# Layer 1's activation rows: low part first, a gap between the parts, rows 2560 bytes apart, and low weights displaced by 128 bytes

## The chip, the cores and the metric

The kernel runs on one core of one Trainium2 chip. The metric is the device time of one execution in microseconds; the kernel before took 2322.99 us (median of three runs, 2322.8 to 2323.42). A profile is one execution recorded by the hardware.

## The reference

A small decoder trunk on 256 tokens with 16 learned prefix tokens in front (272 rows in all), width 2048, two layers, in fp32:

```python
h = jnp.concatenate([meta, x], axis=1)                       # 272 x 2048
# layer 0: forgetting attention
proj = rms_norm(h, norm_attn[0]) @ fox_w_in[0]               # q, k, v, forget gates
h = h + forgetting_attention(q, k, v, cum_logf) @ fox_w_o[0]
h = h + squared_relu_mlp(rms_norm(h, norm_mlp[0]), w_up[0], w_down[0])   # 2048 -> 8192 -> 2048
# layer 1: stick-breaking attention over one shared K/V
k_s, v_s = split(rms_norm(h, kv_norm) @ w_kv)
q = rms_norm(h, norm_attn[1]) @ sb_w_q[0]
h = h + stick_breaking_attention(q, k_s, v_s) @ sb_w_o[0]
h = h + squared_relu_mlp(rms_norm(h, norm_mlp[1]), w_up[1], w_down[1])
out = rms_norm(h, final_norm)[:, 16:]                        # the prefix is dropped
```

Nearly all the arithmetic is in the projections, each an activation matrix times a weight matrix that is read once from memory.

## The kernel before

Activations lie transposed: a feature chunk of 128 features fills the 128 partitions, and the tokens run along a row. There are 16 chunks. Layer 0 works on all 272 tokens. In layer 1 the prefix is needed only for the keys and values, so all its other projections work on 256 tokens; in the code `t0` is 0 for the first kind and 16 (`M`) for the second.

Each fp32 product is made of three products of a faster type, float32r: activations and weights are split into a high part (rounded) and a low part (the rest), and high x high, high weight x low activation, and low weight x high activation are added up; low x low is left out. The class `Split` (L119) holds one such activation matrix: one tile `x_...` of 16 rows per partition, one row for each chunk, with the high and the low part of the chunk in it. `ROWS` (L28) says, in elements of 4 bytes, how far apart rows are and where the parts start: in layer 0 rows are 640 elements apart, the high part starts at 48 and the low part at 368; with 256 tokens rows are 576 apart, the high part starts at 16 and the low part at 272, directly behind it.

`gemm_group` (L182) makes 512 output features of one projection: four accumulators of 128 features, 16 chunks of weights in four blocks `kb` of four chunks. Weights come by DMA into `raw` (two chunks each), ScalarE rounds them into `whi` (L217), VectorE subtracts to get `wlo` (L218). The pool of the weights' parts holds four buffers of each; TensorE then runs the products.

- With all 272 tokens there are three products of 272 elements for each chunk and accumulator (L247 to L249).
- With 256 tokens (`pairs`) the two products with the high weights are one: `sp.both` moves the high and the low activations, 512 elements, in one instruction, and fills the whole accumulator bank of 512 columns, high in the first half and low in the second (L237). The product with the low weights moves the 256 high activations and adds to the first half (L241). At the end `evac` gets both halves and adds them (`residual_add` L254, `total` L258). One accumulator at the very end of layer 1's MLP (`apart`) is made in the first manner.

In blocks 0 and 3 a group runs accumulator by accumulator: four products of 512, then four of 256. In blocks 1 and 2 it runs eight of 512, then eight of 256. Every product loads its weights anew, and the load for the next product runs beside the present one. `gemm_matmul` (L174) pins the order in which products are issued.

All products of all projections are recorded under line L176 of the profile; the accumulator is `acc`, and the names tell the operands: `acc<-x_m,whi` is a high weight by an activation of the up projection, `x_u` the down projection, `x_o` the attention's output projection, `x_a` the first norm's, `x_kv` the shared keys and values.

Where tiles lie: a pool `align` with one tile of 128 bytes stands between the raw weights and their parts. With it `whi`, `wlo` and both `x` buffers begin at multiples of 256 bytes in each partition. An `x` tile is 16 x 640 + 64 elements long, whatever its pitch, and the pool has two buffers of it.

Of the kernel before, what the change touches and what calls it, by code (L numbers as in the profile page):

```python
# [10 lines left out]
F32R = mybir.dt.float32r  # L11
# [4 lines left out]
P = 128  # L16
D = 2048
NC = D // P
M = 16
# [4 lines left out]
QSCALE = 1.0 / math.sqrt(P)  # L24
N_FF = 4


ROWS = {0: (640, 48, 368), M: (576, 16, 272)}  # L28
XROW = 640

G_A0, G_M0, G_KV, G_A1, G_M1, G_FIN = range(6)
# [3 lines left out]
def yoco_kernel(ctx: ExitStack, tc: tile.TileContext, hT_in, gains, b_f, w_f, w_qkv0, w_o0, w_up, w_dn,  # L35
# [7 lines left out]
    wspl = ctx.enter_context(tc.tile_pool(name="wspl", bufs=4))  # L43
# [75 lines left out]
    class Split:  # L119


        def __init__(self, label, t0):
            n = T - t0
            self.t0 = t0
            rows = xs.tile([P, NC * XROW + 64], F32R, tag="x", name=f"x_{label}")
            pitch, hi, lo = ROWS[t0]
            rows = rows[:, hi:hi + NC * pitch].rearrange("p (c t) -> p c t", c=NC)
            self.hi, self.lo = rows[:, :, :n], rows[:, :, lo - hi:lo - hi + n]
            self.both = rows[:, :, :2 * n]

    def split_chunk(sp, gi, c):

# [41 lines left out]
    def gemm_matmul(*args, **kw):  # L174

        ins = nc.tensor.matmul(*args, **kw).ins  # L176
        if queued and pinned[0]:
            tc.add_manual_dep(ins, queued[0].name, mybir.DependencyInfo(mybir.DependencyClass.NoSync,
                                                                        mybir.DependencyReason.DATA))
        queued[:] = [ins]  # L180

    def gemm_group(wblk, sp, t0, evac, before={}, after={}, load_x=None, pairs=False, apart=()):  # L182

        uid[0] += 1
        u = uid[0]
        accs = [pacc.tile([P, 512], F32, tag="acc", name=f"acc_{u}_{m}") for m in range(4)]  # L190
        n = T - t0
        for kb in range(4):
            src_w = wblk[kb].rearrange("p (k c) -> p k c", k=4)
            if kb in before:
                before[kb]()
            piece = 1 if load_x is not None and kb < 2 else 2
            raws = [wraw.tile([P, 2, 512], F32, tag="raw", name=f"raw_{u}_{kb}_{hf}") for hf in range(2)]
            for k0 in range(0, 4, piece):
                if load_x is not None:
                    load_x(range(4 * kb + k0, 4 * kb + k0 + piece))  # L200
                if load_x is not None and kb == k0 == 0:

                    for c0 in (0, 256):
                        nc.scalar.dma_start(raws[0][:, 0, c0:c0 + 256], src_w[:, 0, c0:c0 + 256])
                else:
                    nc.sync.dma_start(raws[k0 // 2][:, k0 % 2:k0 % 2 + piece], src_w[:, k0:k0 + piece])
            parts = []
            for hf in range(2):
                whi = wspl.tile([P, 2, 512], F32R, tag="whi", name=f"whi_{u}_{kb}_{hf}")
                wlo = wspl.tile([P, 2, 512], F32R, tag="wlo", name=f"wlo_{u}_{kb}_{hf}")  # L210
                boxes = [(o, piece, 0, 512) for o in range(0, 2, piece)]
                if load_x is not None and kb == hf == 0:
                    boxes[:1] = [(0, 1, 0, 256), (0, 1, 256, 512)]
                for o, no, c0, c1 in boxes:
                    src = raws[hf][:, o:o + no, c0:c1]
                    hp, lp = whi[:, o:o + no, c0:c1], wlo[:, o:o + no, c0:c1]
                    on_act = nc.scalar.activation(hp, src, AF.Copy)  # L217
                    on_dve = nc.vector.tensor_tensor(out=lp, in0=src, in1=hp.bitcast(F32), op=ALU.subtract)  # L218
                parts.append((whi, wlo))
            if kb in after:  # L220
                with tc.issue_after(on_act.ins), tc.issue_after(on_dve.ins):
                    after[kb]()


            if load_x is not None and kb == 0:
                runs = [([kc], range(4)) for kc in range(4)]
            elif kb in (0, 3):
                runs = [(range(4), [m]) for m in range(4)]
            else:
                runs = [(range(2 * hf, 2 * hf + 2), range(4)) for hf in range(2)]  # L230
            pinned[0] = load_x is None
            for kcs, ms in runs:
                paired = [m for m in ms if pairs and m not in apart]
                single = [m for m in ms if m not in paired]
                for kc in kcs:
                    for m in paired:
                        gemm_matmul(accs[m], parts[kc // 2][0][:, kc % 2, m * P:(m + 1) * P], sp.both[:, 4 * kb + kc],  # L237
                                    start=kb == kc == 0, stop=False)
                for kc in kcs:
                    for m in paired:  # L240
                        gemm_matmul(accs[m][:, :n], parts[kc // 2][1][:, kc % 2, m * P:(m + 1) * P],  # L241
                                    sp.hi[:, 4 * kb + kc], start=False, stop=kb == kc == 3)
                for m in single:
                    for kc in kcs:
                        wh, wl = (w[:, kc % 2, m * P:(m + 1) * P] for w in parts[kc // 2])
                        hi, lo = sp.hi[:, 4 * kb + kc], sp.lo[:, 4 * kb + kc]
                        gemm_matmul(accs[m][:, :n], wh, hi, start=kb == kc == 0, stop=False)  # L247
                        gemm_matmul(accs[m][:, :n], wh, lo, start=False, stop=False)
                        gemm_matmul(accs[m][:, :n], wl, hi, start=False, stop=kb == kc == 3)  # L249
                if kb == 3:  # L250
                    for m in ms:
                        evac(m, [accs[m][:, :n]] + ([accs[m][:, n:]] if m in paired else []))
# [18 lines left out]
    def load_x(chunks):  # L271
        c0, n = chunks[0], len(chunks)
        nc.sync.dma_start(hT[:, c0:c0 + n, :], hT_in[:, c0:c0 + n, :])
        if c0 == 0:
            nc.sync.dma_start(g_sb, gains)
        for c in chunks:
            split_chunk(xa, G_A0, c)
# [86 lines left out]
    for g in range(4):  # L364
# [11 lines left out]
        if g == 0:  # L376

            gemm_group(w_qkv0[0], xa, 0, lambda m, acc, qT=qT: nc.scalar.copy(qT[:, m, :], acc[0]),
                       after={kb: (lambda kb=kb: first_norm(kb)) for kb in range(4)}, load_x=load_x)
            gate_products()  # L380
            box["rstd"] = norm.finish()
            for m in range(4):
                evac_q(m, [qT[:, m, :]])
            forget_gates(box["rstd"])
        else:
            gemm_group(w_qkv0[3 * g], xa, 0, evac_q)
# [4 lines left out]
        def decays(j):  # L391

            for i, (o, n) in enumerate(((0, 144), (144, T))):
                nc.vector.scalar_tensor_tensor(out=s[:, j, o:o + n], in0=fk[:, j, :n],
                                               scalar=fq_sb[:, i, 4 * g + j:4 * g + j + 1],
                                               in1=maskA[:, o:o + n], op0=ALU.subtract, op1=ALU.add)

        gemm_group(w_qkv0[3 * g + 1], xa, 0, lambda m, acc: evac_kv(m, acc, kT),
                   after={j: (lambda j=j: decays(j)) for j in range(4)})

# [255 lines left out]
    a, y, t, rs = (fin[:, i, :] for i in range(4))  # L656
# [81 lines left out]
```

## Time and profile before

| | |
|---|---|
| median of three runs | 2322.99 us (2322.8 to 2323.42) |
| profiled execution | 2323.63 us |
| its span, first to last instruction | 2321.9 us |
| TensorE busy | 2310.8 us |
| VectorE busy | 1350.6 us |
| ScalarE busy | 1064.0 us |
| read from memory | 407.29 MB |
| mean granted TensorE clock | 0.998 |

Span and profiled time differ by 1.7 us, the start and the end outside the instructions. In the rows of the profile PE is TensorE, PEld its weight loads, DVE VectorE, ACT ScalarE. A row of a group names line, engine, operation, output and inputs, their sizes, the count, then busy time in us with the mean duration in ns, then the engine's idle time just before these instructions with what ended it. Matmuls overlap in the pipeline, so the pace is read from the distance of starts in the timeline, or from the number of matmuls in a window.

### The profile page before, as it was taken

Reading aid. Unit: us, or ns where it says so; the run is one execution under the profiler, and the core shown is the slowest. Engines: PE = TensorE matmul, PEld = TensorE weight load, DVE = VectorE, ACT = ScalarE, POOL = GpSimd, SP = SyncE. Lnnn points to the kernel's source line nnn. Section 1 sums busy time; section 2 is a strip of 40 time slices with the busy share of each in tenths; the row PEclk is TensorE's granted clock in tenths of the full one; section 3 lists DMA queues with packets and bytes.
Section 4 is the critical chain, followed back from the end, with each engine's and each line's share of the span. In section 5 each row is a group of like instructions: output and inputs, shape, how many; then the busy total and the mean of one; then the engine's idle time right before and its main releaser. Section 6 shows DMA issues by size and latency. Waiting matters only on the chain.

```text
span 2321.9 us, 39954 instructions
## 1 busy us (share of the span) xinstructions
PE 2310.8 (100%) x16486; PEld 2190.4 (94%) x16486; DVE 1350.6 (58%) x1923; ACT 1064.0 (46%) x1477; POOL 39.9 (2%) x58
## 2 busy tenths in 40 slices
PE   9999999999999999999999999999999999999998
PEld 9999999999999999999998999988888888888887
DVE  7665555655455455445566655567665665665665
ACT  6434344544344344344455444455544543543553
POOL 1000000000000000000000000000000000000000
PEclk9999999999999999999999999999999999999999
DMA  6544444455555455555556444455555555556553
GB/s 233 172 156 165 171 158 173 171 183 173 183 175 183 171 186 176 178 182 171 187 173 200 155 145 146 146 175 186 197 184 193 192 186 198 186 184 199 181 199 127
DMA packets 116630, 412.00 MB, mean 177 GB/s; under 512 B 13264, under 2 KB 16736, under 8 KB 116448
## 3 DMA queue, kind: packets, MB, share of 16 engines
q1 hardware_dynamic: 114560, 406.29, 51.4%
q10 hardware_dynamic: 1888, 3.16, 0.4%
q8 instruction: 129, 2.11, 0.4%
q14 instruction: 53, 0.43, 0.1%
HBM read 407.29 MB, written 2.11 MB: 176 GB/s over the span
## 4 chain that ended last, share of the span: by engine, by line
PE 99%; DMA 0%; DVE 0%; ACT 0%; issue 0%; DVEq 0%; SPq 0%; ACTq 0%
PE acc L176 95%; PE ps L406 0%; PE pza L585 0%; PE pv L339 0%; PE po L468 0%; PE po L624 0%; DMA raw<-w_qkv 0%; PE po L625 0%; PE pzb L586 0%; PE po L469 0%; DMA hT<-hT_in 0%; PE po L626 0%; DVE ob L680 0%; PE pf L306 0%; PE pf L305 0%; PE pta L600 0%
## 5 line engine op out<-in xcount | busy, mean ns | idle before, releaser
L218 DVE TENSOR_TENSOR wlo<-raw,whi 128x1024 fp32r<-128x1024 f32 (+1 forms) x773 | 931.5, 1217 | 746.8 <-ACT whi L217 745.2
L217 ACT ACTIVATE whi<-raw 128x1024 fp32r<-128x1024 f32 (+1 forms) x773 | 799.2, 1050 | 953.9 <-PE acc L176 877.4
L176 PE MATMUL acc<-x_u,whi 128*128 128x272 f32 (+2 forms) x3088 | 647.5, 321 | 0.0
L176 PE MATMUL acc<-x_m,whi 128*128 128x272 f32 (+1 forms) x3072 | 646.1, 322 | 0.0
L176 PEld LDWEIGHTS acc<-x_u,whi 128*128 128x128 f32 x3088 | 499.9, 188 | 26.7
L176 PEld LDWEIGHTS acc<-x_m,whi 128*128 128x128 f32 x3072 | 497.8, 188 | 27.4
L176 PE MATMUL acc<-x_u,wlo 128*128 128x272 f32 (+1 forms) x2048 | 445.9, 282 | 0.0
L176 PE MATMUL acc<-x_m,wlo 128*128 128x272 f32 (+1 forms) x2048 | 443.7, 282 | 0.0
L176 PE MATMUL acc<-x_a,whi 128*128 128x272 f32 (+1 forms) x1792 | 360.6, 306 | 0.4 <-ACT x_a L134 0.2
L176 PEld LDWEIGHTS acc<-x_u,wlo 128*128 128x128 f32 x2048 | 340.3, 188 | 15.7
L176 PEld LDWEIGHTS acc<-x_m,wlo 128*128 128x128 f32 x2048 | 339.5, 188 | 15.9
L176 PEld LDWEIGHTS acc<-x_a,whi 128*128 128x128 f32 x1792 | 284.4, 188 | 9.9 <-issue 0.7
L176 PE MATMUL acc<-x_a,wlo 128*128 128x272 f32 (+1 forms) x1024 | 254.5, 286 | 0.0
L176 PE MATMUL acc<-x_kv,whi 128*128 128x272 f32 x1024 | 194.1, 288 | 0.0
L176 PEld LDWEIGHTS acc<-x_a,wlo 128*128 128x128 f32 x1024 | 179.6, 188 | 4.9 <-issue 0.5
L176 PE MATMUL acc<-x_o,whi 128*128 128x272 f32 (+1 forms) x768 | 162.3, 322 | 0.0
L176 PEld LDWEIGHTS acc<-x_kv,whi 128*128 128x128 f32 x1024 | 160.6, 188 | 0.4
L176 PE MATMUL acc<-x_kv,wlo 128*128 128x272 f32 x512 | 147.3, 288 | 0.0
L256 DVE TENSOR_TENSOR hT<-acc,hT 128x256 f32<-128x256 f32 (+1 forms) x239 | 102.4, 428 | 71.4 <-PE acc L176 69.5
L176 PEld LDWEIGHTS acc<-x_o,whi 128*128 128x128 f32 x768 | 124.3, 188 | 6.8
L176 PE MATMUL acc<-x_o,wlo 128*128 128x272 f32 (+1 forms) x512 | 111.6, 283 | 0.0
L176 PEld LDWEIGHTS acc<-x_kv,wlo 128*128 128x128 f32 x512 | 96.5, 188 | 0.1
(226 smaller groups left out, 1040.0 us busy)
## 6 DMA issues: line engine op xcount, KB each, us to landing
raw<-w_up SPq DMA_DIRECT2D x256, 512.0 KB, 4.7
raw<-w_dn SPq DMA_DIRECT2D x256, 512.0 KB, 4.7
raw<-w_qkv SPq DMA_DIRECT2D x92, 512.0 KB, 3.8
raw<-w_o SPq DMA_DIRECT2D x64, 512.0 KB, 4.5
raw<-w_kv SPq DMA_DIRECT2D x64, 512.0 KB, 3.6
raw<-w_q SPq DMA_DIRECT2D x32, 512.0 KB, 4.6
fk<-f_dram ACTq DMA_DIRECT2D x4, 544.0 KB, 5.0
raw<-w_qkv SPq DMA_DIRECT2D x7, 256.0 KB, 4.8
```

What stands on the lines that cost most here:

```text
L176: ins = nc.tensor.matmul(*args, **kw).ins
L217: on_act = nc.scalar.activation(hp, src, AF.Copy)
L218: on_dve = nc.vector.tensor_tensor(out=lp, in0=src, in1=hp.bitcast(F32), op=ALU.subtract)
L256: nc.vector.tensor_tensor(out=hT[:, c, t0:], in0=a, in1=hT[:, c, t0:], op=ALU.add)
```

## The change

For layer 1's matrices with 256 tokens the low part now comes first, at the row's start (element 0), and the high part starts at element 304, so that a gap of 48 elements lies between them; rows are 640 elements (2560 bytes) apart, as in layer 0. The paired product moves two pieces of 256 elements. Its accumulator now has the low activations' half first, and the low weights' product adds to the second half. A buffer of `wlo` has rows of 576 elements instead of 512; in groups with pairs the 512 weights start 32 elements (128 bytes) into the row, in the others at its beginning. Layer 0's `ROWS` keep their places. The pool of the weights' parts grows by 4 x 512 bytes, and everything allocated behind it moves up by 2048 bytes.

```diff
-ROWS = {0: (640, 48, 368), M: (576, 16, 272)}
+ROWS = {0: (48, 368), M: (304, 0)}
 XROW = 640
...
-            pitch, hi, lo = ROWS[t0]
-            rows = rows[:, hi:hi + NC * pitch].rearrange("p (c t) -> p c t", c=NC)
-            self.hi, self.lo = rows[:, :, :n], rows[:, :, lo - hi:lo - hi + n]
-            self.both = rows[:, :, :2 * n]
+            hi, lo = ROWS[t0]
+            o = min(hi, lo)
+            rows = rows[:, o:o + NC * XROW].rearrange("p (c t) -> p c t", c=NC)
+            self.hi, self.lo = (rows[:, :, k - o:k - o + n] for k in (hi, lo))
+
+            d = abs(lo - hi)
+            if t0:
+                self.both = rows[:, :, :2 * d].rearrange("p c (i t) -> p c i t", i=2)[:, :, :, :n]
+            self.low_first = lo < hi
...
-                wlo = wspl.tile([P, 2, 512], F32R, tag="wlo", name=f"wlo_{u}_{kb}_{hf}")
+                wlo = wspl.tile([P, 2, 576], F32R, tag="wlo", name=f"wlo_{u}_{kb}_{hf}")
+                wlo = wlo[:, :, 32:544] if pairs else wlo[:, :, :512]
...
-                        gemm_matmul(accs[m][:, :n], parts[kc // 2][1][:, kc % 2, m * P:(m + 1) * P],
+                        gemm_matmul(accs[m][:, n:] if sp.low_first else accs[m][:, :n],
+                                    parts[kc // 2][1][:, kc % 2, m * P:(m + 1) * P],
                                     sp.hi[:, 4 * kb + kc], start=False, stop=kb == kc == 3)
```

## The prediction

> **What bounds the kernel now.** I read the page first (busy times, chain), then TensorE's waits, then the groups by shape, and last the timeline of TensorE, where the pace of single forms shows. The page:
>
> ```profile
> span 2321.9 us, 39954 instructions
> ...
> PE 2310.8 (100%) x16486; PEld 2190.4 (94%) x16486; DVE 1350.6 (58%) x1923; ACT 1064.0 (46%) x1477; POOL 39.9 (2%) x58
> ...
> PE 99%; DMA 0%; DVE 0%; ACT 0%; issue 0%; DVEq 0%; SPq 0%; ACTq 0%
> ```
>
> TensorE is busy from end to end, and 99% of the chain that ended last is its own work. Its whole waiting, in the view of waits of that engine:
>
> ```profile
> PE pr_fin L669 <- DVE fin L663: 1.3, 1, 1.3
> PE idle L62 <- DVE mean_w L58: 1.1, 1, 1.1
> PE pms_fin L637 <- ACT sq_fin L649: 0.2, 1, 0.2
> PE acc L176 <- ACT x_a L134: 0.2, 1, 0.2
> ```
>
> That is 2.8 us, of which 0.2 us lies in the products of L176. So no transfer, split or eviction sets the time; only the pace at which TensorE takes one matmul after another does, and the change can act on the time only through that pace. The groups by shape give the counts of the forms that the change touches, the paired ones (x_m, x_u, x_o, x_a of layer 1; 512 elements moved by a high weight, 256 by a low one), and the two operations that split the weights:
>
> ```profile
> L218 DVE TENSOR_TENSOR wlo<-raw,whi 128x1024 fp32r<-128x1024 f32 x764 | 925.5, 1223 | 744.4 <-ACT whi L217 742.9
> ...
> L176 PE MATMUL acc<-x_m,whi 128*128 128x512 f32 x1024 | 266.8, 393 | 0.0
> L176 PE MATMUL acc<-x_u,whi 128*128 128x512 f32 x1008 | 262.6, 392 | 0.0
> ...
> L176 PE MATMUL acc<-x_u,wlo 128*128 128x256 f32 x1024 | 152.5, 278 | 0.0
> L176 PE MATMUL acc<-x_m,wlo 128*128 128x256 f32 x1024 | 150.4, 278 | 0.0
> ...
> L176 PE MATMUL acc<-x_o,whi 128*128 128x512 f32 x256 | 67.2, 393 | 0.0
> L176 PE MATMUL acc<-x_a,whi 128*128 128x512 f32 x256 | 66.9, 393 | 0.0
> ```
>
> The durations there (393 and 278 ns) overlap, since matmuls are pipelined; the pace has to come from starts. There are 1024 + 1008 + 256 + 256 = 2544 paired products of 512, and one low-weight product of 256 goes with each. The first window below lies in layer 1, the second in layer 0 (us; busy, instructions; clock; DMA):
>
> ```profile
> 1800.00:2200.00 400.00, 400.00 (x2311) 1.00 0.56 190
> 700.00:1100.00 400.00, 400.00 (x3246) 1.00 0.52 179
> ```
>
> In layer 1 one matmul takes 400 / 2311 = 173.1 ns on average, so one pair (a 512 and a 256) 346.2 ns; in layer 0 a 272-wide one takes 400 / 3246 = 123.2 ns. The granted clock is 1.00 in both. The pairs are 2544 x 0.3462 = 881 us, 38% of the span. The timeline of TensorE in one group of layer 1 (start us, length, instructions; the length includes the pipeline's tail, so I use differences of starts):
>
> ```profile
> 1622.00 0.62 PE L176 MATMUL acc<-x_m,wlo 128*128 128x256 f32 x4
> 1622.45 1.07 PE L176 MATMUL acc<-x_m,whi 128*128 128x512 f32 x4
> 1623.37 0.63 PE L176 MATMUL acc<-x_m,wlo 128*128 128x256 f32 x4
> 1623.84 1.09 PE L176 MATMUL acc<-x_m,whi 128*128 128x512 f32 x4
> ...
> 1626.60 2.00 PE L176 MATMUL acc<-x_m,whi 128*128 128x512 f32 x8
> 1628.45 1.10 PE L176 MATMUL acc<-x_m,wlo 128*128 128x256 f32 x8
> 1629.39 2.00 PE L176 MATMUL acc<-x_m,whi 128*128 128x512 f32 x8
> 1631.23 1.11 PE L176 MATMUL acc<-x_m,wlo 128*128 128x256 f32 x8
> ```
>
> Two things are to be seen. Sixteen 512s take 1.85 + 1.84 us, 230.6 ns each, so on average 346.2 - 230.6 = 115.6 ns are left for a 256. And the 256s have two paces in the same code: four in 0.45 us (112.5 ns), then four in 0.47 us (117.5 ns), and eight in 0.94 us (117.5 ns). The pace of a form is thus not fixed, though its rows lie alike; something at its start picks it.
>
> **The change, part by part.** Each engine's instructions stay in number, order and waits; what moves are addresses and the form of some operands.
>
> *Distances of whole 256 bytes.* The pitch of a row goes from 2304 to 2560 bytes (9 and 10 times 256), a wlo slot from 4096 to 4608, and all tiles behind the slots by 2048. The trace holds such a shift: x_m and x_u lie in the pool's two buffers, (16 x 640 + 64) x 4 = 41216 = 161 x 256 bytes apart. The same stretch of a group that reads x_u:
>
> ```profile
> 1737.44 2.00 PE L176 MATMUL acc<-x_u,whi 128*128 128x512 f32 x8
> 1739.28 1.10 PE L176 MATMUL acc<-x_u,wlo 128*128 128x256 f32 x8
> 1740.22 2.00 PE L176 MATMUL acc<-x_u,whi 128*128 128x512 f32 x8
> 1742.06 1.11 PE L176 MATMUL acc<-x_u,wlo 128*128 128x256 f32 x8
> ```
>
> 1.84, 0.94 and 1.84 us, as for x_m. So such shifts cost 0, and layer 0, whose operands move by nothing else, keeps its 123.2 ns.
>
> *The subtraction writes wlo with a gap.* L218 wrote 1024 elements in a row and now writes 2 x 512. A row in which VectorE writes two pieces of 256:
>
> ```profile
> L361 DVE TENSOR_TENSOR x_o<-po,x_o 128x512 fp32r<-128x512 f32 x16 | 11.1, 692 | 20.3 <-ACT x_o L360 20.3
> ```
>
> Two of these are 1384 ns against 1223, so a subtraction costs between 0 and +161 ns. It hides under TensorE: VectorE stood idle 744.4 us before these subtractions, waiting for whi, and TensorE waited for none of them beyond the 0.2 us above. I take 0; without that cover it would be up to 764 x 0.161 = 123 us, but the idle time is six times that.
>
> *Evictions.* The low-weight products now add to the second half of the accumulator, not the first. Both halves are one tile, released by the same last product, so L256, L262 and L263 run at the same times: 0.
>
> *The paired operand is now two pieces.* Before, 512 elements in one run; now 256, a skip of 48 elements, 256. Layer 1's attention moves two pieces of the same type, 416 elements apart:
>
> ```profile
> 1332.15 0.40 PE L600 MATMUL pta<-eh,ntri_r 128*128 128x512 f32 x1
> 1332.38 0.29 PE L604 MATMUL ptb<-eh,ntri_r 128*128 128x288 f32 x1
> ...
> 1333.50 0.40 PE L601 MATMUL pta<-el,ntri_r 128*128 128x512 f32 x1
> 1333.73 0.29 PE L602 MATMUL pta<-eh,nones_r 128*128 128x288 f32 x1
> 1333.86 0.30 PE L603 MATMUL pta<-el,nones_r 128*128 128x288 f32 x1
> 1334.00 0.29 PE L605 MATMUL ptb<-el,ntri_r 128*128 128x288 f32 x1
> 1334.13 0.29 PE L176 MATMUL acc<-x_kv,whi 128*128 128x272 f32 x1
> ```
>
> The 512s take 0.23 us, no more than the unbroken ones to the 10 ns that single rows resolve. The three 288s in a row take 1334.13 - 1333.73 = 0.40 us, 133.3 ns each; an unbroken 288 at layer 0's pace would take 123.2 x 288 / 272 = 130.4 ns. One break then costs 2.9 ns. I take that, since three in a row resolve better than single ones: 2544 x 2.9 ns = +7.4 us. Ends: 0 from the 512s, +7.4 from the 288s.
>
> *Where the rows start against the weights.* Modulo 256 bytes, before: whi and wlo at 0, both activation parts at 64. After: whi at 0, wlo at 128, low part at 0, high part at 192. So a pair starts at 0 against its weights instead of 64, and the low-weight product stays at 64 (192 - 128). No row shows a start at 0. For the 512 the ends are two of the fastest 256s, 225.0 ns (2544 x -5.6 = -14.2 us), and the pace per element of the broken 288s, 133.3 x 512 / 288 = 237.0 ns (+6.4 ns, +16.3 us, the break within it). For the 256 they are the two paces, 112.5 and 117.5 against the mean of 115.6: -7.9 to +4.8 us. Between ends on both sides of the present pace I take 0, the present pace being nearest to both.
>
> [...]
>
> **Sum.** +7.4 us from the break, 0 from the rest. The profiled execution took 2323.63 us (span 2321.9), so it would take 2331.0; the median of the runs is 2322.99, 0.6 us below, so I predict 2330.4 us, +0.32%. A difference of 0.2%, 4.6 us, is about what can be told from no change.
>
> **Rivals.**
>
> *Faster: the fast pace of the low-weight products becomes the rule.* The start of a run picks between 112.5 and 117.5 ns, and new ends of the pairs before it could always pick the first, while a break in mid-operand costs nothing, as the 512s of L600 and L601 have it. That gives 2322.99 - 7.9 = 2315.1 us. For it: both paces occur already, next to each other. Against it: nothing says which start the new pairs leave. It decides against my forecast once the break costs less than 3.1 ns and the fast pace holds throughout. Lower still, with the pairs half way to 225 ns as well (-7.1), lies 2308.
> [...]
>
> *No change.* TensorE reads a row without regard to where it starts, and the skip is free: 2323.0 us, within 4.6 us. For it: the equal times of x_m and x_u, and the 0.23 us of the broken 512s. Against it: equal times were shown for shifts of whole 256 bytes alone. [...]
>
> *Much slower: starting level with the weights collides.* Pair and whi now start at the same place modulo 256, a case that no row has. If each 512 goes at 237.0 ns and each 256 at its slow 117.5: +16.3 + 4.8 = +21.1 us, 2344.1 us. Against it: the next weight load starts alongside every product already, without a wait of TensorE in the profile.
>
> **How the numbers follow.** Forecast (break paid, paces kept) 0.38, with its own range from 2328 to 2335; faster 0.32; no change 0.16; much slower 0.14. A small part of the forecast's case falls under 0.2%: faster 0.32, same 0.17, slower 0.51. The range for 8 in 10 runs from 2311 to 2341: it leaves out the lower tail of the faster case and the most of the much slower one.
>
> **What would show it right or wrong.** After the change, eight 512s of one group in the timeline should take 1.87 us (233.5 ns) where they took 1.85 and 1.84, and the 256s still show 112.5 and 117.5 ns mixed. The window in the middle of layer 1 should count 2292 matmuls in 400 us instead of 2311 (349.1 ns a pair), that of layer 0 still 3246. If the 512s keep 1.84 us, the break is free; if the 256s all run at one pace, the starts matter, which I priced at 0; if layer 0 moves, a shift of whole 256 bytes is not neutral; if TensorE waits for wlo, the gap in the subtraction costs more than its cover. Any of these makes the prediction wrong in the step named.

## The result: 7 us slower, as many as forecast, and not where forecast

The changed kernel takes 2330.04 us (median of 8 runs, 2329.54 to 2331.78) against 2323.02 for the kernel before on the same chip: a ratio of 1.0031, 95% interval 1.0020 to 1.0042. The forecast was 2330.4. The page of the changed kernel, its busy times and its chain:

```profile
span 2330.1 us, 39954 instructions
...
PE 2317.9 (99%) x16486; PEld 2197.0 (94%) x16486; DVE 1351.1 (58%) x1923; ACT 1064.1 (46%) x1477; POOL 39.1 (2%) x58
...
PE 99%; DMA 1%; DVE 0%; ACT 0%; issue 0%; DVEq 0%; ACTq 0%; SPq 0%
```

TensorE is busy 7.1 us longer (2317.9 against 2310.8) and is still 99% of the chain. Its waits in the products:

```profile
PE acc L180 <- ACT whi L222: 1.2, 2, 0.9
...
PE acc L180 <- ACT x_a L138: 0.2, 1, 0.2
```

The 1.2 us are two waits in the first 20 us, in layer 0, that the profile of before does not have. They are part of why this one execution took 2331.78 us, 1.7 above the median. The windows in layers 1 and 0:

```profile
1800.00:2200.00 400.00, 400.00 (x2292) 1.00 0.58 189
700.00:1100.00 400.00, 400.00 (x3245) 1.00 0.54 178
```

Layer 0 keeps its pace (3245 against 3246 matmuls), and layer 1 falls from 2311 to 2292, 349.0 ns a pair. That is the number the prediction named. The groups by shape show that it comes about otherwise:

```profile
L180 PE MATMUL acc<-x_m,whi 128*128 128x512 f32 x1024 | 267.4, 393 | 0.0
L180 PE MATMUL acc<-x_u,whi 128*128 128x512 f32 x1008 | 263.2, 393 | 0.0
L180 PE MATMUL acc<-x_u,wlo 128*128 128x256 f32 x1024 | 154.7, 281 | 0.0
L180 PE MATMUL acc<-x_m,wlo 128*128 128x256 f32 x1024 | 152.6, 281 | 0.0
```

The products that now move two pieces last 393 ns (393 and 392 before). It is the low-weight products, whose operand has no break, that go from 278 to 281 ns. The timeline of the group shown before (same instructions):

```profile
1624.73 0.64 PE L180 MATMUL acc<-x_m,wlo 128*128 128x256 f32 x4
1625.20 1.09 PE L180 MATMUL acc<-x_m,whi 128*128 128x512 f32 x4
1626.13 0.64 PE L180 MATMUL acc<-x_m,wlo 128*128 128x256 f32 x4
1626.61 1.09 PE L180 MATMUL acc<-x_m,whi 128*128 128x512 f32 x4
...
1629.40 2.01 PE L180 MATMUL acc<-x_m,whi 128*128 128x512 f32 x8
1631.25 1.11 PE L180 MATMUL acc<-x_m,wlo 128*128 128x256 f32 x8
1632.19 2.01 PE L180 MATMUL acc<-x_m,whi 128*128 128x512 f32 x8
1634.05 1.11 PE L180 MATMUL acc<-x_m,wlo 128*128 128x256 f32 x8
```

Eight 512s take 1.85 and 1.86 us, not the 1.87 foretold. The runs of four 256s take 0.47 and 0.48 us, where before every other one took 0.45: the fast pace is gone there. Taken over all products in the two traces, as the mean distance from one start to the next, a 512 went from 230.16 to 230.98 ns and a 256 from 116.46 to 118.34: 2544 x 0.82 = 2.1 us and 2544 x 1.88 = 4.8 us, 6.9 us together.

### The profile page after: what moved, and what is told of

It is laid out like the page before. It is cut to its first block, busy times and chain, and to the rows that moved or that the text cites. A ratio compares the mean times of both kernels' runs of the same rounds, so it can differ in the third digit from the quotient of the medians.

```text
span 2330.1 us, 39954 instructions
## 1 busy us (share of the span) xinstructions
PE 2317.9 (99%) x16486; PEld 2197.0 (94%) x16486; DVE 1351.1 (58%) x1923; ACT 1064.1 (46%) x1477; POOL 39.1 (2%) x58
## 4 chain that ended last, share of the span: by engine, by line
PE 99%; DMA 1%; DVE 0%; ACT 0%; issue 0%; DVEq 0%; ACTq 0%; SPq 0%
PE acc L180 95%; DMA hT<-hT_in 1%; PE ps L412 0%; PE pza L591 0%; PE pv L345 0%; PE po L474 0%; PE po L630 0%; PE pzb L592 0%; PE po L631 0%; DMA g_sb<-gains 0%; PE po L475 0%; PE po L632 0%; DVE ob L686 0%; PE pf L311 0%; PE pf L312 0%; PE pta L606 0%
```

## The experiments

All kernels below compute the same function. What they vary are three places modulo 256 bytes, always against the weights loaded for the product: where the first piece of the paired operand starts, where the second piece starts, and where the low-weight product's operand starts (the table gives the three in bytes). Four theories were set against each other. A is the prediction: the break between the pieces costs, the starts do not. B: each product's own start sets its pace. C: unlike starts of the parts cost. D: starts at an even multiple of 64 bytes (0, 128) are dear, at an odd one (64, 192) cheap.

All times are medians, with the ratio to the kernel before in the same batch and its interval (its median was 2323.52 us in the batch of the e runs, 2323.54 in that of the f runs and 2323.30 in that of the g runs and h1); the paces are mean distances of starts over all such products of the trace.

| kernel | first, second, low | us | ratio (95%) | 512, ns | 256, ns |
|---|---|---|---|---|---|
| before | 64, 64, 64 | 2323.02 | | 230.16 | 116.46 |
| changed | 0, 192, 64 | 2330.04 | 1.0031 (1.0020 to 1.0042) | 230.98 | 118.34 |
| e1_break | 64, 64, 64 | 2323.68 | 1.0001 (0.9991 to 1.0010) | 230.16 | 116.46 |
| e4_shift | 64, 64, 64 | 2323.38 | 0.9998 (0.9989 to 1.0008) | 230.15 | 116.46 |
| e2_wlo128 | 64, 64, 192 | 2329.26 | 1.0024 (1.0015 to 1.0034) | 232.29 | 116.62 |
| e3_rows | 0, 192, 192 | 2328.55 | 1.0023 (1.0014 to 1.0032) | 230.24 | 118.29 |
| f1_at0 | 0, 0, 0 | 2333.13 | 1.0040 (1.0026 to 1.0055) | 231.47 | 118.82 |
| f2_at128 | 128, 128, 128 | 2334.94 | 1.0047 (1.0032 to 1.0062) | 231.86 | 119.11 |
| f3_at192 | 192, 192, 192 | 2324.81 | 1.0004 (0.9994 to 1.0014) | 232.67 | 114.35 |
| f4_lo0_hi64 | 0, 64, 64 | 2333.03 | 1.0041 (1.0026 to 1.0056) | 232.83 | 117.46 |
| g1_lo64_hi192 | 64, 192, 192 | 2320.43 | 0.9988 (0.9978 to 0.9997) | 231.95 | 113.49 |
| g2_hi64_lo192 | 64, 192, 64 | 2331.75 | 1.0037 (1.0024 to 1.0050) | 231.85 | 118.05 |
| g3_hi192_lo64 | 192, 64, 192 | 2337.34 | 1.0061 (1.0046 to 1.0076) | 233.14 | 118.84 |
| h1_weights64 | 0, 0, 0 | 2332.34 | 1.0039 (1.0025 to 1.0053) | 231.47 | 118.83 |

### The break alone

```diff
-ROWS = {0: (640, 48, 368), M: (576, 16, 272)}
+ROWS = {0: (640, 48, 368), M: (640, 16, 336)}
```

The paired operand is two pieces with 256 bytes between them; the code that builds it is that of the changed kernel.

> The kernel before with the break alone: high part at 16 as before, low part at 336 behind a gap of 64 elements (256 bytes), rows 640 apart, so every start keeps its place modulo 256 bytes; wlo not displaced. Theory A (the prediction: the break costs 2.9 ns in each of 2544 pairs, the starts nothing): +7.4 us, 2330.4, the 512s at 233.5 ns, the 256s at 115.6 with both paces. Theory B (the starts modulo 256 set the pace, the break is free): 2323.0 within 1 us, all paces as before.

Theory A falls. The timeline of the same group:

```profile
1626.88 2.00 PE L182 MATMUL acc<-x_m,whi 128*128 128x512 f32 x8
1628.73 1.10 PE L182 MATMUL acc<-x_m,wlo 128*128 128x256 f32 x8
1629.67 2.00 PE L182 MATMUL acc<-x_m,whi 128*128 128x512 f32 x8
1631.51 1.11 PE L182 MATMUL acc<-x_m,wlo 128*128 128x256 f32 x8
1632.45 0.39 PE L182 MATMUL acc<-x_m,whi 128*128 128x512 f32 x1
```

1.85, 0.94, 1.84 us and 0.94 to the next run: what the kernel before shows. Over all 2544 pairs a 512 takes 230.16 ns and a 256 116.46 with the break as without it, and the time is 2323.68 us against 2323.52: the break costs nothing.

### Shifts of whole 256 bytes

```diff
-ROWS = {0: (640, 48, 368), M: (576, 16, 272)}
+ROWS = {0: (640, 48, 368), M: (640, 16, 272)}
...
-                wlo = wspl.tile([P, 2, 512], F32R, tag="wlo", name=f"wlo_{u}_{kb}_{hf}")
+                wlo = wspl.tile([P, 2, 576], F32R, tag="wlo", name=f"wlo_{u}_{kb}_{hf}")
+                wlo = wlo[:, :, 0:512]
```

> The kernel before with shifts of whole 256 bytes alone: layer 1's rows 640 elements apart instead of 576, rows of wlo 576 instead of 512 without a displacement, all tiles behind moved by 2048 bytes. Theories A and B both expect 2323.0 within 1 us and every pace as before; if it is slower, addresses above 256 bytes or the written gap of wlo matter.

It came out so: the row pitch of 2560 bytes, the longer wlo slots with the gap that VectorE writes, and the tiles moved by 2048 bytes cost nothing (2323.38 us against 2323.52; 230.15 and 116.46 ns against 230.16 and 116.46).

### The two halves of the change

The displacement of wlo alone, activations as before:

```diff
-                wlo = wspl.tile([P, 2, 512], F32R, tag="wlo", name=f"wlo_{u}_{kb}_{hf}")
+                wlo = wspl.tile([P, 2, 576], F32R, tag="wlo", name=f"wlo_{u}_{kb}_{hf}")
+                wlo = wlo[:, :, 32:544] if pairs else wlo[:, :, 0:512]
```

> The kernel before with wlo alone displaced by 128 bytes in the paired groups (rows of wlo 576 elements), activations as before. The low-weight product then starts at 192 instead of 64 against its weights. Theory A: 2323.0, no change. Theory B: the 256s change their pace, somewhere from 112.5 to 120 ns, so -8 to +11 us; the 512s before another 512 keep 230.6 ns.

And the rows alone, low part first, with wlo at the beginning of its rows of 576 elements (the accumulator's halves change places as in the changed kernel):

```diff
-ROWS = {0: (640, 48, 368), M: (576, 16, 272)}
+ROWS = {0: (640, 48, 368), M: (640, 304, 0)}
```

> The changed kernel without the displacement of wlo: low part at 0, high part at 304, wlo at the beginning of its rows of 576 elements. Theory A: +7.4 us, 2330.4, as in the changed kernel, all of it in the 512s. Theory B: the 512s as in the changed kernel (they see the same starts), the 256s another pace than its 118.4 ns, because they start at 192 instead of 64 against wlo: from 2319 to 2334.

Each is slower by itself, 5.7 and 5.0 us above the 2323.52 of this batch, and the two together by 7.0: they do not add up. With wlo displaced:

```profile
1622.77 0.63 PE L182 MATMUL acc<-x_m,wlo 128*128 128x256 f32 x4
1623.24 1.10 PE L182 MATMUL acc<-x_m,whi 128*128 128x512 f32 x4
1624.17 0.63 PE L182 MATMUL acc<-x_m,wlo 128*128 128x256 f32 x4
...
1627.46 2.03 PE L182 MATMUL acc<-x_m,whi 128*128 128x512 f32 x8
1629.33 1.11 PE L182 MATMUL acc<-x_m,wlo 128*128 128x256 f32 x8
```

The 512s, whose moving rows and own weights had not moved, went from 230.16 to 232.29 ns. Taken by place in the run, over the runs of four and eight in the trace, the last 512 went from 228.6 to 235.8 ns and the others from 230.5 to 231.4. Beside that last one the displaced wlo of the next product is loaded, and it makes up 3.4 of the 5.4 us that all 512s lost. Theory B had the 512s before another 512 unchanged; they moved less, by 0.9 ns, but they moved. So a product's pace depended here on more than its own start. The 256s kept their mean, but only as a mean: for x_m and x_u the runs of four went from 116.1 to 117.9 ns a product, and the runs of eight from 116.8 to 115.2.

With the rows alone, a run of four and a run of eight:

```profile
1621.34 1.08 PE L182 MATMUL acc<-x_m,whi 128*128 128x512 f32 x4
1622.26 0.64 PE L182 MATMUL acc<-x_m,wlo 128*128 128x256 f32 x4
1622.74 1.08 PE L182 MATMUL acc<-x_m,whi 128*128 128x512 f32 x4
...
1626.94 2.00 PE L182 MATMUL acc<-x_m,whi 128*128 128x512 f32 x8
1628.78 1.10 PE L182 MATMUL acc<-x_m,wlo 128*128 128x256 f32 x8
1629.71 2.00 PE L182 MATMUL acc<-x_m,whi 128*128 128x512 f32 x8
```

Four 512s take 0.92 us and four 256s 0.48 us, 120 ns each, slower than either pace of before. Eight 256s take 0.93 us, so the last four of them, in 0.45 us, run at the faster pace again. The 512s keep 230.24 ns, and the 256s carry the whole loss: theory A had it all in the 512s. Theory B expected the 256s at another pace than in the changed kernel, and their mean is the same (118.29 and 118.34 ns).

### Unbroken rows at the other places

One line of each of three kernels (the code that builds the operands is that of e1_break, which for unbroken rows makes the operand of before):

```diff
-ROWS = {0: (640, 48, 368), M: (576, 16, 272)}
+ROWS = {0: (640, 48, 368), M: (576, 0, 256)}
+ROWS = {0: (640, 48, 368), M: (576, 32, 288)}
+ROWS = {0: (640, 48, 368), M: (576, 48, 304)}
```

> The kernel before with layer 1's rows moved 64 bytes down: high part at 0, low part at 256 elements, unbroken, wlo not displaced; every start is 0 modulo 256, like whi and wlo. Theory B (each product's own start against its weights sets its pace): a level start is no better than in the rows with the low part at 0, so 512s at 230 to 232 ns, 256s anywhere from 113 to 120, 2316 to 2336. Theory C (what costs is that the parts and the two kinds of weights no longer start alike, not where): 2323.0 within 1 us, because all still start alike. Theory A is out and expects 2323.0.

> As the kernel before, with layer 1's unbroken rows starting at 128 modulo 256 (high part at element 32, low part at 288). Theory B: another pace of both forms, 2316 to 2336. Theory C: 2323.0 within 1 us.

> As the kernel before, with layer 1's unbroken rows starting at 192 modulo 256 (high part at 48, low part at 304). The low-weight products then start at 192 against wlo, as where low part lies at 0 and high part at 304 without a displaced wlo, which had 118.3 ns. Theory B: 256s at 118.3 ns again, +4.7 us from them, about 2328. Theory C: 2323.0 within 1 us.

Rows at 0 and at 128 are 9.6 and 11.4 us slower, rows at 192 within 1.3 us of the kernel before. Theory C expected no change in all three and falls. At 192 the 256s ran at 114.35 ns, not the 118.3 foretold by theory B from the rows of the changed kernel: the same start against wlo, after another paired product, gives another mean. The place in the run shows what lies behind it. For x_m and x_u in the runs of eight, the last three 256s take 113.3 to 113.4 ns each in e3_rows as in f3_at192. The first ones differ: 116.7, 121.6, 123.2 and 118.3 ns in e3_rows, 118.4 and then 113.4 in f3_at192. So for these two kernels theory B describes the pace at which a run settles (113.3 to 113.4 ns), and lacks the products before it settles. The runs at 0, 128 and 192 led to theory D.

### Against the weights, or in memory

```diff
-                whi = wspl.tile([P, 2, 512], F32R, tag="whi", name=f"whi_{u}_{kb}_{hf}")
-                wlo = wspl.tile([P, 2, 512], F32R, tag="wlo", name=f"wlo_{u}_{kb}_{hf}")
+                whi = wspl.tile([P, 2, 576], F32R, tag="whi", name=f"whi_{u}_{kb}_{hf}")
+                whi = whi[:, :, 16:528] if pairs else whi[:, :, 0:512]
+                wlo = wspl.tile([P, 2, 576], F32R, tag="wlo", name=f"wlo_{u}_{kb}_{hf}")
+                wlo = wlo[:, :, 16:528] if pairs else wlo[:, :, 0:512]
```

The activations stay; both weights move by 64 bytes.

> The kernel before with whi and wlo both displaced by 64 bytes in the paired groups, activations where they were (64 modulo 256 in memory, 0 against the weights). If the start against the weights counts: as with unbroken rows at 0, 512s at 231.4 and 256s at 118.8 ns, about 2333. If the place in memory counts by itself: 2323.5 and every pace as before.

The time is 2332.34 us: it is the place against the weights that counts. The group with the weights moved:

```profile
1627.91 2.00 PE L182 MATMUL acc<-x_m,whi 128*128 128x512 f32 x8
1629.75 1.12 PE L182 MATMUL acc<-x_m,wlo 128*128 128x256 f32 x8
1630.70 2.00 PE L182 MATMUL acc<-x_m,whi 128*128 128x512 f32 x8
```

and with the activations moved to 0 instead (f1_at0):

```profile
1627.60 2.00 PE L182 MATMUL acc<-x_m,whi 128*128 128x512 f32 x8
1629.44 1.12 PE L182 MATMUL acc<-x_m,wlo 128*128 128x256 f32 x8
1630.39 2.00 PE L182 MATMUL acc<-x_m,whi 128*128 128x512 f32 x8
```

1.84 and 0.95 us in both: 118.8 ns a 256, and the same means over all products to 0.01 ns.

### Mixed starts

Low part at 0, high part at 64:

```diff
-ROWS = {0: (640, 48, 368), M: (576, 16, 272)}
+ROWS = {0: (640, 48, 368), M: (640, 272, 0)}
```

> Low part first at 0, high part at element 272 (64 modulo 256), rows 640 apart, wlo not displaced: the pair starts level with whi as in the changed kernel, the low-weight product at 64 against wlo as in both kernels. Theory B: 512s at 230.0 ns as with the low part at 0 and the high at 304, 256s at 116.5 as before, so 2323 within 2 us. Theory C: slower, 2326 to 2330, since the parts do not start alike. If the 256s lie at 118 ns here too, it is the pair ahead that sets them, not their own start.

2333.03: the time is not where B put it (2323), nor in C's range (to 2330). Restoring the low product's start, and with it the second piece's, made it 4.5 us worse than in e3_rows, by the medians of two batches whose kernel before agrees to 0.02 us. The traces say the same: a pair takes 232.83 + 117.46 = 350.29 ns here and 348.53 there, 1.76 ns more in each of 2544 pairs.

Then the same rows as in e3_rows with the low part at 64 instead of 0:

```diff
-ROWS = {0: (640, 48, 368), M: (640, 304, 0)}
+ROWS = {0: (640, 48, 368), M: (640, 304, 16)}
```

> The changed rows without the displacement of wlo, but the low part at element 16 (64 modulo 256) instead of 0; the high part stays at 304 (192). The low part is still first, there is still a gap, rows 640 apart. Theory D (a start is dear where it is an even multiple of 64 bytes against the weights, 0 or 128, and cheap at an odd one, 64 or 192; order and gap are free): all starts are odd, so 2323 to 2325, against 2328.6 with the low part at 0. Theory C (parts that start unlike cost): 2327 to 2330.

```profile
1621.00 0.62 PE L182 MATMUL acc<-x_m,wlo 128*128 128x256 f32 x4
1621.45 1.09 PE L182 MATMUL acc<-x_m,whi 128*128 128x512 f32 x4
1622.38 0.62 PE L182 MATMUL acc<-x_m,wlo 128*128 128x256 f32 x4
...
1625.59 2.02 PE L182 MATMUL acc<-x_m,whi 128*128 128x512 f32 x8
1627.44 1.07 PE L182 MATMUL acc<-x_m,wlo 128*128 128x256 f32 x8
1628.35 2.02 PE L182 MATMUL acc<-x_m,whi 128*128 128x512 f32 x8
1630.20 1.07 PE L182 MATMUL acc<-x_m,wlo 128*128 128x256 f32 x8
```

Here the 256s run at the fast pace throughout: four in 0.45 us, eight in 0.91 us, 113.5 ns on average; the 512s pay 1.8 ns each for it (231.95). This kernel, with the low part first and a gap, takes 2320.43 us, 0.9988 of the kernel before (0.9978 to 0.9997), and beats both. Theory D had the direction, but the time lies 2.6 us below its range; theory C (2327 to 2330) is out. Against e3_rows the low part's start moved by 64 bytes (and a wlo slot is 4096 bytes again, a shift of whole 256 bytes, which cost nothing in e4_shift); that is worth 8.1 us (2328.55 to 2320.43).

Two more with all starts odd, the high part in front:

```diff
-ROWS = {0: (640, 48, 368), M: (576, 16, 272)}
+ROWS = {0: (640, 48, 368), M: (640, 16, 304)}
+ROWS = {0: (640, 48, 368), M: (640, 48, 336)}
```

> The kernel before with the low part moved to element 304 (192 modulo 256), high part at 16 (64) in front. Theory D: 2322 to 2325, all starts odd. Theory C: 2326 to 2330. If the second piece's start does not matter at all, every pace is as before and the time 2323.5.

> High part in front at element 48 (192 modulo 256), low part at 336 (64), wlo not displaced. Theory D: 2320 to 2325; the 256s start at 192 against wlo and run at 113.3 ns once settled, as they did with unbroken rows at 192; if the 512s also keep 230 ns, the pair takes 344.5 and the time is 2319. Theory C: 2326 to 2330.

Theory D missed both: 2331.75 and 2337.34, the latter the slowest of all; they lie above C's range too. In g2_hi64_lo192 the paired operand lies as in g1_lo64_hi192, 64 then 192, but the low product starts at 64. The 512s have the same mean (231.85 and 231.95), while the 256s have 118.05 against 113.49. The order of the parts, and with it the halves of the accumulator, differs between these two kernels as well. No run swaps the order alone; from e3_rows to g1_lo64_hi192, where the low part is first in both, the start by itself is worth 8.1 us.

## Why the prediction was right in its number and wrong in its step

- *TensorE's pace is all that the change can act on:* right. 99% of the chain is TensorE's, the added busy time, 7.1 us, is what lies between the medians (7.0 us), and layer 0 kept its pace (3245 matmuls in 400 us against 3246).
- *Distances of whole 256 bytes, the gap in the subtraction, the evictions at 0:* right, the first two by e4_shift (2323.38 us against 2323.52; the subtraction with the gap takes 1224 ns in the changed kernel against 1223) and the last by the changed kernel, where TensorE has no new wait for them: its 1.2 us of new waits are for whi.
- *"One break then costs 2.9 ns", +7.4 us:* wrong, this is the step that failed. By e1_break it costs nothing (230.16 ns with and without). The 133.3 ns of the three broken 288s came from one stretch of 0.40 us read in steps of 0.01 us, which is 130 to 137 ns a product, so a difference of 2.9 ns lay within the rounding. In full, over the eight such stretches of the trace, they take 132.7 ns on average against 130.6 for an unbroken 288 by the pace of layer 0's window, and the broken 512s of L600 and L601 take 232.5 against 230.16. These products are thus some 2 ns slower, and the wrong step was to put that down to the break. They differ from the unbroken ones in more: the two pieces start 128 bytes apart modulo 256, where each unbroken product has one start, and the 288s also write their output in two pieces. What makes them slow stays open; no run isolated it.
- *Where the rows start against the weights, 0:* wrong, this is where the 7 us are. The 0 was the author's estimate, the present pace as the one nearest to both ends, and no row of the profile before has a start at 0. With the weights alone moved by 64 bytes (h1_weights64) the kernel takes 9.0 us more (2332.34 against 2323.30), while TensorE stays busy for all 400.00 us of the window from 1800 to 2200, so no wait accounts for it there. The ends given were -14.2 to +16.3 us for the 512s and -7.9 to +4.8 for the 256s. The measured +2.1 lies well within the first, and the +4.8 just reaches the second: at 118.34 ns the 256s are slower than the 117.5 that was taken as their slow pace, and the sum still fits only because their mean before was 116.46 and not 115.6. Setting the starts to 0 and the break to 7.4 gave the sum by chance.
- *What would show it:* the prediction said that the 512s should go to 233.5 ns and the 256s keep both paces. The 512s went to 230.98, the runs of four 256s lost the fast pace. By the window alone, 2292 matmuls as foretold, the wrong step would have passed for right.
- *The rival "faster":* what it supposed occurs. In g1_lo64_hi192 the fast pace of the 256s is the rule (113.49 ns), and by e1_break the break is free; it gains 2.9 us and not 7.9, since the 512s become slower (231.95 ns against 230.16). The change's own starts do not bring it about.
- *The rivals "no change" and "much slower":* the skip is free (e1_break, 2323.68 us against 2323.52) and shifts of whole 256 bytes are too (e4_shift, 2323.38 against 2323.52), as the first supposed, but TensorE does regard where a row starts (f1_at0, 2333.13 against 2323.54). The second fails by its size: starting level with whi, the 512s take 230.98 ns, and 231.47 with unbroken rows at 0, not 237.0.

Along the runs, the change comes apart so: low part first, gap, and high part at 192 would gain 2.9 us with the low part at 64 (g1_lo64_hi192); the low part at 0 loses 8.1 (e3_rows); the displacement of wlo loses another 1.5 (2328.55 to 2330.04, two batches whose ratios' intervals overlap, so the last step is not settled by the times; the traces' pairs, 348.53 and 349.32 ns, point the same way).

What the mechanism inside TensorE is stays open. Open, too, is which weights count, a product's own or those loaded beside it for the next: whi and wlo lie alike modulo 256 in all kernels but the changed one and e2_wlo128, and in both the last 512 of a run is slower than without the displacement (235.8 against 228.6 ns, and 231.7 against 229.2 in e3_rows), which points at the latter without showing it. Two regularities hold in all 14 kernels: each that has an even start of the first piece is at 2328.55 or more; and of those with an odd one, the five at 2324.81 or less have the second piece and the low product at the same start, the three at 2329.26 or more do not. Both were read off afterwards and tried by no run of their own; a first piece at 128 occurs in one kernel only.

## What to carry to other kernels

Where matmuls stream back to back and each loads new weights, treat the place of the moving rows against the weights, modulo 256 bytes, as a tuning parameter, worth up to 0.7% here (2320.43 to 2337.34 us), and measure whole kernels: the sequence of forms counted, and the mean paces of single forms did not carry over from one layout to another (a 256 that starts at 192 against wlo took 118.29 ns in e3_rows and 114.35 in f3_at192). When a forecast's total comes out, check the groups that were to carry it, since two wrong terms can add up to the right time. A price read off rows that differ in more than one respect may belong to any of them, and a difference smaller than the rounding of the view is no price at all; a layout with only that one respect changed is cheap to run.

## What the runs showed of the hardware that was not expected

- A skip of 256 bytes in the middle of a moving operand cost nothing: 230.16 ns for 512 elements with it (e1_break) or without it.
- TensorE's pace depended on the moving rows' start against the weights, not on their place in memory: moving the rows by 64 bytes (f1_at0) or the weights (h1_weights64) gave the same 231.47 ns a 512 and 118.8 ns a 256, against 230.16 and 116.46. Shifts of whole 256 bytes changed nothing (e4_shift, 230.15 and 116.46 ns). Over the layouts tried, the time ranged from 2320.43 to 2337.34 us, 0.7%, with the same instructions in the same order and count.
- A product's pace depended on its neighbours. Displacing wlo by 128 bytes slowed the 512s, whose moving rows and own weights had not moved, by 2.1 ns on average (e2_wlo128), most of it in the last 512 before the low-weight products (228.6 to 235.8 ns).
- Runs of equal products settled. With the low-weight operand at 192 and wlo in its old place, the last three 256s of a run of eight (x_m, x_u) take 113.3 to 113.4 ns in four kernels (e3_rows, f3_at192, g1_lo64_hi192, g3_hi192_lo64), after up to five slower ones; at 0 (f1_at0, h1_weights64) they take 120.0 ns, at 64 between 116.2 and 119.6. The means over runs of different length hide this: 118.29 ns in e3_rows, 114.35 in f3_at192, 113.49 in g1_lo64_hi192, 118.84 in g3_hi192_lo64.
